# State space outputs of two channel blocks made together on the two column halves of the PE array

## The chip, the cores and the metric

The kernel runs on one core of a Trainium2 chip. The metric is the device time of one execution in microseconds (us). Times below are those of the kernel before, from three runs, and from one profiled execution with its trace.

## What is computed

The reference is one hybrid decoder block over 16 learned meta tokens and 512 tokens of width 1024: a half SwiGLU, then attention (sliding window, 16 query heads on 4 key heads, a sink per head) beside a state space layer, both gated and merged, then a second half SwiGLU and a last norm. Cut to what matters here:

```python
q, k, v, u, g_attn, g_ssm = jnp.split(hn @ w_in[i], SPLITS, axis=-1)
attn = sliding_window_attention(q, k, v, attn_sinks[i])
y = s5_ssm(u, ...)          # 32 groups of 16 channels, 64 complex states each
y = jax.nn.gelu(y)
ssm = (y @ ssm_glu_a[i]) * jax.nn.sigmoid(y @ ssm_glu_b[i])
merged = jax.nn.sigmoid(g_attn) * attn + jax.nn.sigmoid(g_ssm) * ssm
h = h + merged @ w_out[i]
```

The change touches only the end of `s5_ssm`, the GELU behind it, and the transposes that bring `y` into the layout in which the gated unit (`ssm_glu_a`, `ssm_glu_b`) reads it.

## The kernel before

All large products are made of units: 128 output columns against all tokens, as 24 steps. A weight tile is split into two parts (`whi` on ACT, line 173, `wlo` on DVE, line 174), the activations likewise (`hgh`, `hgl`), and three of the four partial products are summed in PSUM (`mm3`, line 238). A unit over all 528 columns of tokens has two matmuls of 264 columns a step; a unit over the 512 real tokens has one of 512. `step` issues a unit's matmuls, then the split of the weights for the unit two ahead (`prep_piece`), then the unit's evacuation. `mids` is a list of calls that go out between the matmuls of a unit, at evenly spaced cuts: with two of them after steps 8 and 16, with three after 6, 12 and 18. The schedule is written by hand: each engine runs its instructions in the order in which the program issues them.

The state space layer works by chunks of 8 time steps (T = 8, 64 chunks of real tokens) and by four blocks of 8 groups (128 channels, `b` from 0 to 3). For each block:

- `ssm_r(b)` brings the inputs `u` back from DRAM as `U`, with time step and channel on the partitions.
- `ssm_c(b)` makes the chunks' inputs to the states (`psS`, line 943, 8 fp32 matmuls, one for each group) and copies them to `SR` and `SI` on ACT.
- `ssm_d_(b)` runs the recurrence over the chunks on DVE and POOL; its last four instructions write the states `X` (lines 980 and 981, even groups, then odd groups).
- `ssm_e(b)` makes the outputs. For each group, two fp32 matmuls add up in `psY`: the inputs `U` against `Mt` (line 992) and the states `X` against `Qt` (line 993). The stationary operand has 64 columns, one for each chunk, so the output stands on 64 partitions. Four groups fill a PSUM bank, and ACT applies the GELU into `Y` (line 994), 64 partitions x 512.
- `ssm_f(b)` transposes `Y` back to channels on partitions, 8 transposes of 64 x 128 (`psT`, line 1002), and splits the result into `YH` (ACT, line 1004) and `YL` (DVE, line 1005), which the gated units read later.

These calls are spread as `mids` over the units `u(2)`, `u(3)`, `k(0)`, `k(1)`, `v(0)`, `v(1)`, `q0(0)`, `q0(1)` by the table `plan` (line 1041). The last `ssm_f(3)` stands behind the last unit, and the attention stage follows: there ACT and DVE split the keys (`KH`, `KL`, lines 1100 to 1104), ACT and POOL the queries (`qs`, lines 1129 and 1130), and the first scores (`ps_s`, line 1152) need all of these.

Tiles of `psS`, `psY` and `psT` come from one PSUM pool of four banks (`ax_ps`). `Y` has one buffer, `X` two, `U` four.

Of the kernel before, what the change touches and what calls it, by code (L numbers as in the profile page):

```python
# [60 lines left out]
def fr(ap):  # L61
    return ap.bitcast(F32)
# [3 lines left out]
def hybrid_block_kernel(  # L66
# [134 lines left out]
    def step2(ua, ub, mids=()):  # L201
        """Two units of which the last tile of operands comes late: it goes last in both."""
        a, b = ua[0](*take(), None), ub[0](*take(), None)
        next(a)
        for m in mids:
            m()
        prep_piece()
        next(b)
        for g in (a, b):
            for _ in g:  # L210
                pass
        ua[1]()
        prep_piece()
        ub[1]()
# [8 lines left out]
    def accumulate(seq, emit, mids):  # L223
        """One accumulation group; the callables in mids go out between its matmuls."""
# [126 lines left out]
    def ffn_units(hg, hT, n528, mm_ps, g_p, t_p, chunks, last_hook=None, first_mm=None, tail=False):  # L351
        """The units of one half-residual SwiGLU, hT += 0.5 * its output; with tail, the last chunk's
        down projection is left out and its operands are returned."""
# [118 lines left out]
    def ssm_params(ps_p):  # L472
# [114 lines left out]
        # the even groups' rows stay on the lower partitions, the odd ones' on the upper  # L587
# [145 lines left out]
    # the tensor engine's clock rises while the first loads are under way  # L733
# [27 lines left out]
    def x_in(h, d):  # L761
        """Block columns d of token half h: the transpose, then the two parts one and two blocks later."""
# [14 lines left out]
    def first_mm(p, hi, lo, mids):  # L777
        """The first two units take the first half of the tokens first, while the second is brought in."""
# [118 lines left out]
    def ev_u(b):  # L897
        """Step-major u: [channel, (step, chunk)], the two chunks of meta tokens first; by way of DRAM
        it comes back as [(7 - step, channel of the group), (group, chunk)]."""
# [84 lines left out]
    def ssm_e(b):  # L984
        u, xs = su.pop(b), sxs.pop(b)
        y = s_p.tile([64, T, GB, 16], F32, tag="Y", name="Y")
        for h in range(2):
            ps = ax_ps.tile([128, 512], F32, tag="ax", name="psY")
            for i in range(4):
                g = GB * b + 4 * h + i  # L990
                o = ps[:64, 128 * i:128 * i + 128]
                PE.matmul(out=o, lhsT=u[:, 4 * h + i, 2:NCH], rhs=Mt[:, g, :], start=True, stop=False)  # L992
                PE.matmul(out=o, lhsT=xs[:, 4 * h + i, :], rhs=Qt[:, g, 1:T + 1, :].rearrange("p t c -> p (t c)"), start=False, stop=True)  # L993
            S.activation(out=y[:, :, 4 * h:4 * h + 4, :].rearrange("k t g c -> k g t c"),
                         in_=ps[:64, :].rearrange("k (g t c) -> k g t c", g=4, t=T), func=AF.Gelu_apprx_tanh)
        sy[b] = y

    def ssm_f(b):
        y = sy.pop(b)
        ps = ax_ps.tile([128, 512], F32, tag="ax", name="psT")  # L1000
        for t in range(T):
            PE.transpose(ps[:, 64 * t:64 * t + 64], y[:, t].rearrange("k g c -> k (g c)"), ident[:64, :64])
        src = ps.rearrange("p (t k) -> p k t", t=T)
        S.activation(out=YH[:, b, :].rearrange("p (k t) -> p k t", t=T), in_=src, func=AF.Copy)
        V.tensor_tensor(out=YL[:, b, :].rearrange("p (k t) -> p k t", t=T), in0=src,
                        in1=fr(YH[:, b, :]).rearrange("p (k t) -> p k t", t=T), op=ALU.subtract)
# [27 lines left out]
    def go(f, b):  # L1034
        return lambda: f(b)
# [10 lines left out]
        (unit528(ev_v(0)), [(ssm_d_, 1), (ssm_c, 2), (ssm_e, 0)]),  # L1046
        (unit528(ev_v(1)), [(ssm_d_, 2), (ssm_c, 3), (ssm_e, 1), (ssm_f, 0)]),
        (unit512(ev_q0(0)), [(ssm_d_, 3), (ssm_e, 2), (ssm_f, 1)]),
        (unit512(ev_q0(1)), [(ssm_e, 3), (ssm_f, 2)]),
# [3 lines left out]
    ssm_f(3)  # L1053
# [31 lines left out]
    # masks, with the sign that the negated scores need  # L1085
# [6 lines left out]
    # hm[p, h]: 1 where row p of the stacked meta probabilities belongs to head h  # L1092
# [78 lines left out]
    def s2(n, c, kb):  # L1171
        """One block of keys: the probabilities' transpose."""
# [188 lines left out]
    # the last chunk's down projection by halves of the tokens, each half's norm behind the products  # L1361
# [115 lines left out]
```

## Time and profile before

| what | value |
|---|---|
| median of three runs | 1161.07 us (1159.37, 1161.07, 1162.34) |
| profiled execution, first to last instruction (span) | 1160.7 us |
| mean granted TensorE clock | 0.991 |
| DMA over the span | 108.42 MB, 93 GB/s |
| the eight GELUs (line 994) | 0.59 us each |
| the four `YH` copies, the four `YL` subtractions | 0.58 and 0.69 us each |

No other time is listed for the profiled execution than its span, which lies within the three runs' times.

In the rows of a timeline the columns are the start in us from the span's start, the duration, the engine, the line, the operation, output and inputs by the program's names, the part of the array (rows * columns), the shapes, how many were merged into the row, and in brackets how long the engine sat idle before and who ended it. PE is TensorE's matmuls, PEld its weight loads, DVE VectorE, ACT ScalarE, POOL GpSimd. One fp32 matmul of the program shows as two records with a weight load each; a transpose, and a matmul of the split (fp32r) parts, shows as one. Ends of matmuls overlap with the next one's start, so the cost of a group is read from starts, not from durations.

### The profile page before, as it was taken

The numbers are of one execution on the slowest core, as the hardware profiler recorded it, in microseconds if no ns is written. First come the engines' busy times: TensorE is split into PE (matmuls) and PEld (weight loads), VectorE is DVE, ScalarE is ACT, GpSimd is POOL, SyncE is SP. The second block draws the span as 40 slices with busy tenths as digits, with TensorE's granted clock in tenths as the row PEclk, the third lists the DMA queues.
The fourth block names the chain that finished last, engine by engine and source line by source line (L and its number), as shares of the span: only waits on it lengthen the run. The fifth ranks groups of instructions, "written<-read, shape, count | busy, mean of one in ns | idle before, by whom it ended". The sixth has DMA issues, their size and how long they took to land.

```text
span 1160.7 us, 17253 instructions
## 1 busy us (share of the span) xinstructions
PE 1141.6 (98%) x7022; PEld 1016.8 (88%) x7022; DVE 632.1 (54%) x956; ACT 410.4 (35%) x719; POOL 361.5 (31%) x488
## 2 busy tenths in 40 slices
PE   9999999999999999999999999999999999999997
PEld 7999999999999999987778778878888888888887
DVE  5446653645444363767776777564544444444454
ACT  5322232232222242446565464353322222232234
POOL 1966662543685030425454331021000000000003
PEclk7999999999999999999999999999999999999999
DMA  5533233322423246121122222432333223323221
GB/s 158 115 96 109 73 92 94 91 84 83 110 74 101 69 144 191 48 73 60 51 73 73 73 68 79 145 109 73 108 109 110 73 82 103 112 86 117 84 73 73
DMA packets 105582, 108.42 MB, mean 93 GB/s; under 512 B 7504, under 2 KB 101968, under 8 KB 105376
## 3 DMA queue, kind: packets, MB, share of 16 engines
q1 hardware_dynamic: 103104, 100.74, 27.8%
q0 software_dynamic: 2352, 6.52, 2.2%
q8 instruction: 55, 0.90, 0.3%
q14 instruction: 23, 0.19, 0.1%
q10 hardware_dynamic: 48, 0.07, 0.0%
HBM read 100.80 MB, written 5.34 MB: 91 GB/s over the span
## 4 chain that ended last, share of the span: by engine, by line
PE 88%; DVE 4%; ACT 3%; POOL 2%; issue 2%; DMA 1%; POOLq 0%; DVEq 0%; SPq 0%; ACTq 0%
PE p L238 58%; PE p L412 11%; PE p L414 8%; PE p L798 2%; PE p L1372 1%; DMA hT<-h_keep 1%; ACT E L1157 1%; POOL m L1200 1%; POOL E L1168 1%; PE psK L656 1%; PE psY L992 1%; DVE wlo L174 1%; PE ps_x L744 1%; PE psY L993 1%; PE psS L943 1%
## 5 line engine op out<-in xcount | busy, mean ns | idle before, releaser
L238 PE MATMUL p<-hgh,whi 128*128 128x264 f32 (+1 forms) x1408 | 403.4, 333 | 0.1
L238 PE MATMUL p<-hgl,whi 128*128 128x264 f32 (+1 forms) x1408 | 402.4, 332 | 0.0
L238 PE MATMUL p<-hgh,wlo 128*128 128x264 f32 (+1 forms) x1408 | 400.9, 331 | 0.5 <-DVE wlo L174 0.5
L174 DVE TENSOR_TENSOR wlo<-raw,whi 128x1024 fp32r<-128x1024 f32 (+2 forms) x192 | 254.0, 1323 | 104.5 <-ACT whi L173 102.2
L238 PEld LDWEIGHTS p<-hgh,whi 128*128 128x128 f32 x1408 | 238.5, 188 | 26.0 <-issue 1.5
L238 PEld LDWEIGHTS p<-hgh,wlo 128*128 128x128 f32 x1408 | 238.2, 188 | 24.6 <-DVE wlo L174 1.0
L238 PEld LDWEIGHTS p<-hgl,whi 128*128 128x128 f32 x1408 | 238.4, 188 | 22.4
L173 ACT ACTIVATE whi<-raw 128x1024 fp32r<-128x1024 f32 (+2 forms) x192 | 187.5, 979 | 133.1 <-PE p L414 72.2
L1388 POOL TENSOR_TENSOR acc<-acc,zq 128x256 f32<-128x256 f32 x12 | 8.9, 738 | 349.8 <-ACT zq L1381 349.7
L384 ACT ACTIVATE t<-t 128x528 f32<-128x528 f32 (+1 forms) x44 | 28.1, 639 | 164.3 <-DVE t L383 164.3
L394 ACT ACTIVATE gh<-t 128x528 fp32r<-128x528 f32 (+1 forms) x44 | 28.1, 639 | 159.2 <-DVE t L393 159.2
L432 DVE SCALAR_TENSOR_TENSOR hT<-p,hT 128x528 f32<-128x528 f32 (+1 forms) x56 | 39.1, 698 | 82.8 <-PE p L414 52.2
L412 PE MATMUL p<-gh,whi 128*128 128x264 f32 x352 | 72.8, 288 | 0.7 <-DVE hT L432 0.5
L412 PE MATMUL p<-gl,whi 128*128 128x264 f32 x352 | 71.5, 284 | 0.0
L412 PE MATMUL p<-gh,wlo 128*128 128x264 f32 x352 | 71.4, 284 | 0.0
L383 DVE TENSOR_TENSOR t<-p,r_bc 128x528 f32<-128x528 f32 (+1 forms) x44 | 30.7, 698 | 70.4 <-PE p L238 67.3
L393 DVE TENSOR_TENSOR t<-p,t 128x528 f32<-128x528 f32 (+1 forms) x44 | 30.7, 698 | 63.8 <-PE p L238 63.5
L412 PEld LDWEIGHTS p<-gh,whi 128*128 128x128 f32 x352 | 54.4, 188 | 2.3 <-issue 1.2
L414 PE MATMUL p<-gh,whi 128*128 128x512 f32 x144 | 56.0, 389 | 0.0
L414 PE MATMUL p<-gl,whi 128*128 128x512 f32 x144 | 56.0, 389 | 0.0
L414 PE MATMUL p<-gh,wlo 128*128 128x512 f32 x144 | 56.0, 389 | 0.0
L412 PEld LDWEIGHTS p<-gl,whi 128*128 128x128 f32 x352 | 54.6, 188 | 0.0
(322 smaller groups left out, 1516.1 us busy)
## 6 DMA issues: line engine op xcount, KB each, us to landing
raw<-in_ffn_w_dram SPq DMA_DIRECT2D x42, 1024.0 KB, 5.4
raw<-in_ffn_w_dram SPq DMA_DIRECT2D x24, 768.0 KB, 4.3
raw<-in_w_in_dram SPq DMA_DIRECT2D x16, 1024.0 KB, 5.5
raw<-in_ffn_w_dram SPq DMA_DIRECT2D x12, 512.0 KB, 3.5
raw<-in_w_out_dram SPq DMA_DIRECT2D x4, 1024.0 KB, 8.7
h_keep<-hT POOLq DMA_DIRECT2D x1, 2112.0 KB, 7.3
raw<-in_ssm_glu_a_dram SPq DMA_DIRECT2D x4, 512.0 KB, 3.6
raw<-in_ssm_glu_b_dram SPq DMA_DIRECT2D x4, 512.0 KB, 4.6
```

What stands on the lines that cost most here:

```text
L173: S.activation(out=hi, in_=src, func=AF.Copy)
L174: V.tensor_tensor(out=lo, in0=src, in1=fr(hi), op=ALU.subtract)
L238: PE.matmul(out=o, lhsT=w[:, k0 + k, :], rhs=sl(r, k), start=start, stop=stop)
L383: V.tensor_tensor(out=t1, in0=cell[1], in1=rb(), op=ALU.mult)
L384: S.activation(out=t1, in_=t1, func=AF.Silu)
L393: V.tensor_tensor(out=t3, in0=cell[3], in1=cell["t1"], op=ALU.mult)
L394: S.activation(out=gh, in_=t3, func=AF.Copy)
L412: PE.matmul(out=p[:, h, :HALF], lhsT=wt[:, k, :], rhs=gs[k][c][:, h, :], start=start, stop=stop)
L414: PE.matmul(out=p, lhsT=wt[:, k, :], rhs=gs[k][c].rearrange("p h c -> p (h c)"), start=start, stop=stop)
L432: V.scalar_tensor_tensor(out=hv(hT, d), in0=cell["p"], scalar=0.5, in1=hv(hT, d), op0=ALU.mult, op1=ALU.add)
L656: PE.matmul(out=ps[:16, 128 * i:128 * i + 128], lhsT=BB[:, 0, g, :], rhs=Qt[:, g, 0:T, :].rearrange("p t c -> p (t c)"), start=True, stop= ...
L798: PE.matmul(out=p[:, h, :HALF], lhsT=w[:, k, :], rhs=r[:, k, h * HALF:(h + 1) * HALF], start=(n == 0), stop=(n == 3 * ND - 1))
```

## The change

`ssm_e` now takes two neighbouring blocks, `b0` and `b0 + 1`. For each group of the pair it issues four matmuls: the `U` product of the first block, that of the second, the `X` product of the first, that of the second. The first block's output goes to PSUM partitions 0 to 63, that of the second to 64 to 127, which puts the two on the two column halves of the array (tiles of 128 rows x 64 columns, at columns 0 and 64). One GELU then covers both blocks on 128 partitions, and `Y` has 128 partitions. `ssm_f` takes a pair and one half `q` of the time steps: four transposes of 128 x 128, then for each of the two blocks one copy and one subtraction of 256 elements a partition. The calls move in `plan`: `ssm_e(0)` from `v(0)` to the first cut of `v(1)`, ahead of `ssm_d_(2)`; both halves of `ssm_f` for the first pair to `q0(0)`; `ssm_e(2)` to the middle of `q0(1)`; both halves for the second pair behind the last unit. Comments and docstrings are dropped as well, which alters nothing that runs.

```diff
-    def ssm_e(b):
-        u, xs = su.pop(b), sxs.pop(b)
-        y = s_p.tile([64, T, GB, 16], F32, tag="Y", name="Y")
+    def ssm_e(b0):
+        bs = (b0, b0 + 1)
+        us, xss = [su.pop(b) for b in bs], [sxs.pop(b) for b in bs]
+        y = s_p.tile([128, T, GB, 16], F32, tag="Y", name="Y")
         for h in range(2):
             ps = ax_ps.tile([128, 512], F32, tag="ax", name="psY")
             for i in range(4):
-                g = GB * b + 4 * h + i
-                o = ps[:64, 128 * i:128 * i + 128]
-                PE.matmul(out=o, lhsT=u[:, 4 * h + i, 2:NCH], rhs=Mt[:, g, :], start=True, stop=False)
-                PE.matmul(out=o, lhsT=xs[:, 4 * h + i, :], rhs=Qt[:, g, 1:T + 1, :].rearrange("p t c -> p (t c)"), start=False, stop=True)
+                gi = 4 * h + i
+                for first in (True, False):
+                    for e in range(2):
+                        g = GB * bs[e] + gi
+                        o = ps[64 * e:64 * e + 64, 128 * i:128 * i + 128]
+                        if first:
+                            PE.matmul(out=o, lhsT=us[e][:, gi, 2:NCH], rhs=Mt[:, g, :], start=True, stop=False, skip_group_check=True)
+                        else:
+                            PE.matmul(out=o, lhsT=xss[e][:, gi, :], rhs=Qt[:, g, 1:T + 1, :].rearrange("p t c -> p (t c)"),
+                                      start=False, stop=True, skip_group_check=True)
             S.activation(out=y[:, :, 4 * h:4 * h + 4, :].rearrange("k t g c -> k g t c"),
-                         in_=ps[:64, :].rearrange("k (g t c) -> k g t c", g=4, t=T), func=AF.Gelu_apprx_tanh)
-        sy[b] = y
+                         in_=ps.rearrange("k (g t c) -> k g t c", g=4, t=T), func=AF.Gelu_apprx_tanh)
+        sy[b0] = y
 
-    def ssm_f(b):
-        y = sy.pop(b)
+    def ssm_f(b0, q):
+        y = sy[b0]
         ps = ax_ps.tile([128, 512], F32, tag="ax", name="psT")
-        for t in range(T):
-            PE.transpose(ps[:, 64 * t:64 * t + 64], y[:, t].rearrange("k g c -> k (g c)"), ident[:64, :64])
-        src = ps.rearrange("p (t k) -> p k t", t=T)
-        S.activation(out=YH[:, b, :].rearrange("p (k t) -> p k t", t=T), in_=src, func=AF.Copy)
-        V.tensor_tensor(out=YL[:, b, :].rearrange("p (k t) -> p k t", t=T), in0=src,
-                        in1=fr(YH[:, b, :]).rearrange("p (k t) -> p k t", t=T), op=ALU.subtract)
+        for t in range(4):
+            PE.transpose(ps[:, 128 * t:128 * t + 128], y[:, 4 * q + t].rearrange("k g c -> k (g c)"), ident)
+        src = ps.rearrange("p (t e k) -> p e k t", t=4, e=2)
+        for e in range(2):
+            oh = YH[:, b0 + e, :].rearrange("p (k t) -> p k t", t=T)[:, :, 4 * q:4 * q + 4]
+            ol = YL[:, b0 + e, :].rearrange("p (k t) -> p k t", t=T)[:, :, 4 * q:4 * q + 4]
+            S.activation(out=oh, in_=src[:, e], func=AF.Copy)
+            V.tensor_tensor(out=ol, in0=src[:, e], in1=fr(oh), op=ALU.subtract)
...
-        (unit528(ev_v(0)), [(ssm_d_, 1), (ssm_c, 2), (ssm_e, 0)]),
-        (unit528(ev_v(1)), [(ssm_d_, 2), (ssm_c, 3), (ssm_e, 1), (ssm_f, 0)]),
-        (unit512(ev_q0(0)), [(ssm_d_, 3), (ssm_e, 2), (ssm_f, 1)]),
-        (unit512(ev_q0(1)), [(ssm_e, 3), (ssm_f, 2)]),
+        (unit528(ev_v(0)), [(ssm_d_, 1), (ssm_c, 2)]),
+        (unit528(ev_v(1)), [(ssm_e, 0), (ssm_d_, 2), (ssm_c, 3)]),
+        (unit512(ev_q0(0)), [(ssm_d_, 3), (ssm_f, 0, 0), (ssm_f, 0, 1)]),
+        (unit512(ev_q0(1)), [(ssm_e, 2)]),
     ]
...
-    ssm_f(3)
+    ssm_f(2, 0)
+    ssm_f(2, 1)
```

Three places show what moves. The first is PE's queue where the first output block begins (in `v(0)` before); these are rows of the kernel before.

```order
L238 MATMUL p<-hgl,whi 128x264 x2
L238 MATMUL p<-hgh,wlo 128x264 x2
L992 MATMUL psY<-Mt,U 64x128
L993 MATMUL psY<-Qt,X 64x128
L992 MATMUL psY<-Mt,U 64x128
```

And these are rows of PE's queue at the first output block of the changed kernel (in `v(1)`, after six steps), with the semaphores that an instruction waits for.

```order
L238 MATMUL p<-hgl,whi 128x264 x2
L238 MATMUL p<-hgh,wlo 128x264 x2
L999 MATMUL psY<-Mt,U 64x128 [waits DMASW4_49,DMASW5_49,DMASW3_49,DMASW6_49,DMASW2_49,DMASW7_49,DMASW1_49,DMASW0_49] x2
L1001 MATMUL psY<-Qt,X 64x128
L1001 MATMUL psY<-Qt,X 64x128 [waits DVE_49]
L999 MATMUL psY<-Mt,U 64x128 x2
L1001 MATMUL psY<-Qt,X 64x128
```

Instructions of the two blocks now alternate, and the first two that read the second block's states (`X`, even groups, then odd groups) wait for DVE; the waits for DMA are for `Mt`, built long before.

The second place is ACT's queue at the end of the stage, from the last GELUs to the first key splits. Before:

```order
L994 ACTIVATE Y<-psY 64x4x8x16 x2
L1004 ACTIVATE YH<-psT 128x512
L173 ACTIVATE whi<-raw 128x1024
L1004 ACTIVATE YH<-psT 128x512
L1100 ACTIVATE KH<-kT 64x544
```

The same place of ACT's queue in the changed kernel, from the weight split ahead of the last GELUs on:

```order
L173 ACTIVATE whi<-raw 128x1024
L1003 ACTIVATE Y<-psY 128x4x8x16 x2
L173 ACTIVATE whi<-raw 128x1024
L1017 ACTIVATE YH<-psT 128x64x4 x4
L1113 ACTIVATE KH<-kT 64x544
```

Between the last transposes and the first key split stand four copies of 256 elements a partition in place of one of 512.

The third place is DVE's queue between the states of block 2 and those of block 3. Before:

```order
L981 TENSOR_TENSOR X<-a_5386,a_5387 64x4x64
L1005 TENSOR_TENSOR YL<-psT,YH 128x512
L174 TENSOR_TENSOR wlo<-raw,whi 128x1024
L930 TENSOR_TENSOR vT<-p,r_bc 128x528
L961 TENSOR_TENSOR a_5515<-SR,pr 128x264
```

In the changed kernel, from the end of block 3's states on:

```order
L980 TENSOR_TENSOR X<-a_5499,a_5500 64x4x64
L981 TENSOR_TENSOR X<-a_5501,a_5502 64x4x64
L1018 TENSOR_TENSOR YL<-psT,YH 128x64x4 x4
L174 TENSOR_TENSOR wlo<-raw,whi 128x1024
L1042 SCALAR_TENSOR_TENSOR tq_5563<-p,r_bc 128x512
```

The split of the first outputs stood ahead of the recurrence of block 3 (lines 961 to 981) and now stands behind it.

More of the change, by code (lines that the diff above doesn't have):

```diff
@@ L1032, in ev_q0, with go @@
         return f
-    def go(f, b):
-        return lambda: f(b)
+    def go(f, *a):
+        return lambda: f(*a)
     step(*unit528(ev_u(0)), hold=True)
```

## The prediction

> **What bounds the kernel now.** I read the page first: which engine is busy, and what the chain that ended last is made of.
>
> ```profile
> PE 1141.6 (98%) x7022; PEld 1016.8 (88%) x7022; DVE 632.1 (54%) x956; ACT 410.4 (35%) x719; POOL 361.5 (31%) x488
> ...
> PE 88%; DVE 4%; ACT 3%; POOL 2%; issue 2%; DMA 1%; POOLq 0%; DVEq 0%; SPq 0%; ACTq 0%
> ```
>
> TensorE is busy for 98% of the span and makes 88% of the chain. A busy PE is not a PE at its peak, so I then took the table by stage, for the stretch that the change rewrites (from the unit `v(0)` to the last transposes), and the rows of its two tiles.
>
> ```profile
> 469.37:514.33 44.96, 44.96 (x339) 40.08 (x337) 28.17 (x53) 16.50 (x34) 15.74 (x25) 1.00 0.16 48
> ...
> L992 PEld LDWEIGHTS psY<-Mt,U x64: 133/137/137, 475.6 to 508.4; 128*64 128x64 f32 x64
> L992 PE MATMUL psY<-Mt,U x64: 272/273/323, 475.6 to 508.5; 128*64 128x128 f32 x64
> L993 PE MATMUL psY<-Qt,X x64: 272/272/273, 475.9 to 508.7; 128*64 128x128 f32 x64
> L1002 PE MATMUL psT<-ident,Y x32: 221/223/273, 491.2 to 514.2; 64*128 64x64 f32 x32
> ```
>
> In this stretch (columns: length, busy time of PE, PEld, DVE, ACT and POOL, granted clock, DMA share, GB/s) PE never waits and has its full clock, DVE is busy for 28.2 of 45.0 us, ACT for 16.5. So time is won here only by giving PE less to do, and what PE saves reaches the end unless a wait takes its place. `psY` is 128 records on half of the columns (64 fp32 matmuls, two records each); `psT` is 32 records on half of the rows. Next, what one block of each costs inside the stream of ordinary 512-column matmuls:
>
> ```profile
> 495.44 0.40 PE L238 MATMUL p<-hgl,whi 128*128 128x512 f32 x1
> 495.68 0.40 PE L238 MATMUL p<-hgh,wlo 128*128 128x512 f32 x1
> 496.00 0.43 PE L992 MATMUL psY<-Mt,U 128*64 128x128 f32 x2
> 496.27 0.38 PE L993 MATMUL psY<-Qt,X 128*64 128x128 f32 x2
> ...
> 499.33 0.38 PE L993 MATMUL psY<-Qt,X 128*64 128x128 f32 x2
> 499.64 0.50 PE L238 MATMUL p<-hgh,whi 128*128 128x512 f32 x1
> 499.98 0.39 PE L238 MATMUL p<-hgl,whi 128*128 128x512 f32 x1
> ...
> 500.91 0.39 PE L238 MATMUL p<-hgh,wlo 128*128 128x512 f32 x1
> 501.23 0.71 PE L1002 MATMUL psT<-ident,Y 64*128 64x64 f32 x8
> 501.86 0.50 PE L238 MATMUL p<-hgh,whi 128*128 128x512 f32 x1
> 502.20 0.39 PE L238 MATMUL p<-hgl,whi 128*128 128x512 f32 x1
> ```
>
> Ordinary matmuls start 0.23 us apart. From 495.68 to 499.98 lie two such steps (0.46) and one `psY` block: 4.30 - 0.46 = **3.84 us**, four times 15.4. Inside it 28 records start between 496.27 and 499.33: 0.109 each, so 32 take 3.50 and 0.34 goes to entering and leaving. From 500.91 to 502.20: 1.29 - 0.46 = **0.83 us** for a `psT` block, four times 3.3.
>
> **The change part by part.** *Output matmuls.* There are as many as before, 64 instructions or 128 records, now in two blocks of 64 whose instructions alternate between the halves. If the halves run side by side, the time of two records is that of one. It can't be less: the two records of one instruction use the same half and keep their 0.109. A block is then 32 x 0.109 + 0.34 = 3.84, two are 7.7, and 15.4 - 7.7 = **7.7 us** are saved. If nothing overlaps, a block is 64 x 0.109 + 0.34 = 7.34, two are 14.7, and 0.7 is saved (two entries). No row of before shows a second half, so its pitch lies between these ends, or above the upper one if changing halves costs something. One thing that could bind is loading weights:
>
> ```profile
> 496.00 0.19 PEld L992 LDWEIGHTS psY<-Mt,U 128*64 128x64 f32 x2 [0.37 <-issue]
> ...
> 472.29 1.90 PE L943 MATMUL psS<-U,Wt 128*128 128x66 f32 x16
> ```
>
> The first two loads of a block last 0.19 together and one lasts 0.137, so the second began 0.053 after the first; `psS`, with twice the columns to load and short streams, runs at (1.90 - 0.27)/15 = 0.109 a record, again 0.055 for 64 columns. Side by side, two loads fall on every 0.109: just enough. I take the full overlap, since every load in these rows already runs under a matmul of the same rows of the array.
>
> The Trainium skill, "TensorEngine Tiling (Array Packing)", section "Key Properties", says that changing the tiling mode drains the engine, while different tiles run weight loads and matmuls in parallel. For the first this trace has 0.34 us a block; no run here shows the second. Its "TensorE: Matmul & The Clock Gate", "Measured speedup vs the span model", has 2.38 for three column tiles; scaled to two that is 1.59, and my estimate by it is two blocks of 4.74, 5.9 saved in place of 7.7.
>
> *Transposes.* 32 of 64 rows become 16 of 128 x 128. Four such stand elsewhere in the trace:
>
> ```profile
> 154.43 0.41 PE L238 MATMUL p<-hgh,wlo 128*128 128x264 f32 x2
> 154.67 0.60 PE L671 MATMUL psW<-ident,Pb 128*128 128x128 f32 x4
> 155.02 0.49 PE L238 MATMUL p<-hgh,whi 128*128 128x264 f32 x2
> 155.35 0.28 PE L238 MATMUL p<-hgl,whi 128*128 128x264 f32 x1
> ```
>
> From 154.43 to 155.35 lie four ordinary steps of 0.122 (0.49) and the four transposes: 0.43, with no gap at either end. Four groups make 1.7 for 3.3: **1.6 us** saved.
>
> *GELU and the split.* ACT has four GELUs for eight, and eight copies of 256 elements for four of 512; DVE likewise eight short subtractions. Both engines idle beside PE here, so I count nothing, but for the last group (below). The DMA queues and POOL keep their order.
>
> *The new wait.* `ssm_e(0)` now also needs block 1's states, one cut into `v(1)`.
>
> ```profile
> 479.33 0.42 DVE L981 TENSOR_TENSOR X<-a,a 64x256 f32<-64x256 f32 x1
> ```
>
> DVE's order up to there is unchanged, so the last write of block 1's states still ends at 479.75. Before, `psS` of block 2 (472.29) stands 12 steps into `v(0)`, a step being two matmuls of 0.122, 0.243 in all, so `v(0)` starts at 469.37. Without `psY` in it, `v(0)` lasts 24 steps (5.84) and 16 records of `psS` (1.75): to 476.96. Six steps (1.46) and the entry (0.1) lead to 478.5; the first matmul on odd-group states of block 1 comes 0.8 later when overlapped, at 479.3. It waits some **0.5 us**, `psY` and all of `v(1)` behind it. If nothing overlaps, it comes at 480.1 and waits for nothing. The second pair:
>
> ```profile
> 493.55 0.69 DVE L1005 TENSOR_TENSOR YL<-psT,YH 128x512 fp32r<-128x512 f32 x1 [4.46 <-ACT YH L1004]
> 494.50 1.23 DVE L174 TENSOR_TENSOR wlo<-raw,whi 128x1024 fp32r<-128x1024 f32 x1 [0.26 <-ACT whi L173]
> ...
> 502.14 0.42 DVE L981 TENSOR_TENSOR X<-a,a 64x256 f32<-64x256 f32 x1
> 505.31 0.43 PE L992 MATMUL psY<-Mt,U 128*64 128x128 f32 x2
> ```
>
> Before, the states were done at 502.56, 2.75 ahead of PE. PE now comes 7.1 earlier: three blocks (11.5) and two `psT` (1.7) less, one block with its wait (4.3) and two transpose groups (0.9) more, and four steps (0.9) later in its unit. It needs odd states at 505.3 - 7.1 + 0.8 = 499.0. DVE's 4.46 us of waiting for `YH` go, since that split moves behind these states. From the weight split to the last state DVE needs 8.06 (494.50 to 502.56), and by my count it starts that at 490.4, when ACT has finished `psS` of block 3 and the weights: 498.5. I count nothing; 0.5 of margin is thin.
>
> *The end of the stage.* The last transposes now make four short copies on ACT, ahead of attention's key and query splits.
>
> ```profile
> 513.69 0.71 PE L1002 MATMUL psT<-ident,Y 64*128 64x64 f32 x8
> 514.44 0.60 ACT L1004 ACTIVATE YH<-psT 128x512 fp32r<-128x512 f32 x1
> 514.93 0.65 ACT L1100 ACTIVATE KH<-kT 64x544 fp32r<-64x544 f32 x1
> 518.42 9.84 POOL L1130 TENSOR_TENSOR qs<-tq,qs 64x512 fp32r<-64x512 f32 x6 [14.81 <-ACT qs L1129]
> 525.58 0.33 PE L1152 MATMUL ps_s<-KH,qs 128*128 128x144 f32 x1 [0.84 <-POOL qs L1130]
> ```
>
> Before, `KH` starts 1.24 after the first transpose, POOL follows ACT, and PE waits 0.84 for POOL at 525.58. Now the first group is done 0.6 after its start (the 0.60 of `psW` above), and four copies at half of the 0.49 between `YH` and `KH` follow: `KH` at about 1.65, some **0.45 us** later with the gaps between copies, which PE pays there in full. If POOL catches up, it costs nothing.
>
> *Sum*: 7.7 + 1.6 - 0.5 - 0.45 = 8.3 us (7.7 + 1.6 = 9.3 without the two waits). The profiled span is 1160.7 and runs go down to 1159.4, so nothing to speak of lies around it; the median is 0.3 above it. 1161.1 - 8.3 = **1152.8 us**.
>
> **The rivals.** *Half an overlap.* In all rows the next load starts as the matmul before it starts. If the other half's load keeps this rule, a matmul of the other half begins 0.055 late and the next of its own 0.109 after it: four records take 0.33 in place of 0.44. A block is 16 x 0.33 + 0.34 = 5.6, two 11.2: 4.2 saved; with 1.6, a wait of 0.2 and the 0.45, 5.2 in all: 1155.9. For it: no row shows a load more than one matmul ahead. Against: all these rows are loads into the columns that the running matmul uses, and the other half's columns are free.
>
> *The halves take turns.* The change doesn't do what it says: 0.7 + 1.6 - 0.45 = 1.8 saved, 1159.3. For it: nothing in the trace ever ran two matmuls at once.
>
> *Loads wait for the other half.* If a load for one half waits until the other half's matmul has ended, each change of half costs 0.055. There are 31 a block, 62 in all: 3.4 us, 1.6 more than the 1.8: 1162.7. Against: loads here run under matmuls. The Trainium skill, "TensorE: Matmul & The Clock Gate", "The mechanism", has such a rule (a load overlaps a matmul in flight only when the row group differs), and both halves share all rows; for loads of the same tile the trace disagrees (496.00 to 499.33: 0.109 a record, not 0.109 + 0.055).
>
> *Slower: each change of half drains PE* as a change of tile shape does. Entering and leaving cost 0.34, so one change 0.17; 62 cost 10.5 against 1.8: 8.7 slower, **1169.8**. It decides from 0.03 us a change on, where 62 eat the 1.8. For it: every change of shape in these rows has its gap. Against: the shape, 128 x 64, stays the same inside a block.
>
> **How the numbers follow.** Full overlap 0.46, half 0.20, taking turns 0.19, waiting loads 0.06, draining 0.09. About 0.3% (3.5 us) is what a measurement of this kernel can tell from no change: below 1157.6 are the first two, 0.66; within are the next two, 0.25; above is the drain, 0.09. The likeliest gives the time. The range starts from it without the two waits (1151.8) less 0.8 for the spread of runs, 1151.0, and goes up over half an overlap to taking turns (1159.3) with the spread of 1.2: 1160.5. Outside are the last two cases, 0.15.
>
> **What would show it.** Right: `psY` records starting in pairs, a block of about 3.8 us (4.3 with the wait) for twice the work; `psT` groups of 0.43 without gaps; a wait of about 0.5 on DVE's `X` in the first block and none in the second; the wait on POOL's `qs` up from 0.84 to 1.3. Half an overlap: blocks of 5.6. Taking turns: blocks of 7.3, 0.109 a record. Draining: gaps at each change, blocks above 12. The forecast is wrong if the blocks exceed 5, or if they shrink and a wait for `X`, `qs` or weights grows by as much.

## The result, and the profile after

The changed kernel takes 1152.74 us (median of six runs, 1151.1 to 1156.33) where the kernel before, run beside it, takes 1162.02 (1159.37 to 1162.34): a ratio of 0.9926, 95% interval 0.9912 to 0.9941. The two medians differ by 9.3 us; the ratio gives 8.6, and its interval 6.9 to 10.2. One execution of the repeated changed kernel further down ran its matmuls at less than half their pace throughout (2571 us); it was the profiled one, and no number is taken from its profile.

From the page of the changed kernel, the busy times and the chain that ended last:

```profile
PE 1130.5 (98%) x7006; PEld 1006.9 (88%) x7006; DVE 632.7 (55%) x960; ACT 408.8 (36%) x719; POOL 360.5 (31%) x488
...
PE 86%; DVE 5%; ACT 4%; issue 2%; POOL 2%; DMA 0%; POOLq 0%; DVEq 0%; SPq 0%; ACTq 0%
```

PE is busy for 11.1 us less and still bounds the kernel, though 2% of the chain has gone from it to DVE and ACT. The spans of the two profiles (1160.7 and 1150.2) differ by 10.5 us, and not all of that is the change: in the first 20 us both kernels run the same instructions, and the table by windows has another clock for them (before, then after; the granted clock is the third number from the right).

```profile
0.00:20.00 20.00, 17.66 (x71) 13.22 (x72) 9.67 (x21) 11.70 (x24) 3.24 (x14) 0.68 0.71 214
```

```profile
0.00:20.00 20.00, 18.02 (x81) 13.40 (x81) 10.38 (x23) 11.50 (x24) 3.22 (x14) 1.00 0.71 215
```

PE is 3.1 us ahead by 60 us and still 3.2 at 460 us, where the change begins. The clock column points at the reason, but its 1.00 after is too high: there, too, the matmuls begin at a slow pace. A pair of transposes of one kind (`ps_x`) takes 0.63 us while the pace is slow and 0.38 afterwards; in the changed kernel the pace rises at about 16 us, in the kernel before it is still slow at 23.67 (changed kernel, then before).

```profile
15.16 0.63 PE L744 MATMUL ps_x<-ident,xb 128*128 128x128 f32 x2
...
16.48 0.38 PE L744 MATMUL ps_x<-ident,xb 128*128 128x128 f32 x2
```

```profile
23.67 0.63 PE L744 MATMUL ps_x<-ident,xb 128*128 128x128 f32 x2
```

When the pace rises differs from one execution to the next and not with the change: at 460 us the profiles of the experiments stand between 0.8 us ahead of this one and 3.4 behind it, and the kernel before with its keys on POOL (below) is only 0.4 behind. From here on I count in one way: number PE's matmuls from the end of the program, subtract the start times of the same matmul in two traces, and take off what that difference was at 460 us. By this count the changed kernel is **8.6 us** ahead after the rewritten stage, 6.3 after the first 20 us of attention, and 7.3 at the end. The stage itself, from the same first instruction to the same last one as in the window shown of before (44.96):

```profile
466.26:502.66 36.40, 36.16 (x322) 32.81 (x320) 30.27 (x56) 14.58 (x31) 16.56 (x25) 1.00 0.19 59
```

The second output block, in the timeline of the changed kernel (start, duration, engine, line, operation, array tile, shapes, records merged):

```profile
495.00 0.40 PE L238 MATMUL p<-hgh,wlo 128*128 128x512 f32 x1
495.32 0.44 PE L999 MATMUL psY<-Mt,U 128*64 128x128 f32 x4
495.59 0.39 PE L1001 MATMUL psY<-Qt,X 128*64 128x128 f32 x4
495.81 0.39 PE L999 MATMUL psY<-Mt,U 128*64 128x128 f32 x4
...
498.97 0.50 PE L238 MATMUL p<-hgh,whi 128*128 128x512 f32 x1
499.30 0.40 PE L238 MATMUL p<-hgl,whi 128*128 128x512 f32 x1
```

Each row now merges four records (two instructions, one for each half) where it merged two, and the rows still start 0.22 apart: two records in the time of one. The block costs 499.30 - 495.00 - 0.46 = **3.84 us** for twice the work. The first block costs 4.53, since it waits. The wait in the view of the tile `psY`, and the last write of the second pair's states in the timeline:

```profile
  DVE X L981: 0.7, 2
```

```profile
495.21 0.42 DVE L981 TENSOR_TENSOR X<-a,a 64x256 f32<-64x256 f32 x1
```

In the changed kernel, idle time ahead of `psY` that ended with DVE's `X` is 0.7 us in two waits, all in the first block; the second pair's states are done at 495.63, 0.3 after its block began with products that don't need them. The four groups of transposes cost 0.43, 0.45 and, for the last two together, 0.88 (502.97 - 501.63 - 0.46 below): 1.76 for 3.33. Then the end of the stage, from the last ordinary matmul ahead of the last transposes on:

```profile
501.63 0.40 PE L238 MATMUL p<-hgh,wlo 128*128 128x512 f32 x1
501.87 1.04 PE L1012 MATMUL psT<-ident,Y 128*128 128x128 f32 x8
502.50 0.39 ACT L1017 ACTIVATE YH<-psT 128x256 fp32r<-128x256 f32 x1 [1.87 <-PE psT L1012]
502.92 0.42 DVE L1018 TENSOR_TENSOR YL<-psT,YH 128x256 fp32r<-128x256 f32 x1 [0.16 <-ACT YH L1017]
502.97 0.39 PE L238 MATMUL p<-hgl,whi 128*128 128x512 f32 x1
503.38 0.66 ACT L1017 ACTIVATE YH<-psT 128x256 fp32r<-128x256 f32 x2 [0.49 <-DVE YL L1018]
...
504.59 0.39 ACT L1017 ACTIVATE YH<-psT 128x256 fp32r<-128x256 f32 x1 [0.55 <-DVE YL L1018]
504.87 0.65 ACT L1113 ACTIVATE KH<-kT 64x544 fp32r<-64x544 f32 x1
...
511.68 1.95 DVE L174 TENSOR_TENSOR wlo<-raw,whi 128x1024 fp32r<-128x1024 f32 x1 [0.66 <-ACT whi L173]
...
514.66 0.30 PE L1165 MATMUL ps_s<-KH,qs 128*128 128x144 f32 x1 [1.54 <-DVE mn L1168]
```

ACT and DVE take turns on the same `psT` tile: the copy for the second block waits for DVE's subtraction of the first (0.49, 0.55). `KH` starts 3.00 us after the first of the last transposes, where it was 1.24. PE pays first at its third score (`ps_s`, the product with `KH`), 12.79 after those transposes; before it was 10.71 (524.40 - 513.69). At the fourth score about 1.0 of that comes back, because the kernel before waits there 0.84 for `qs` and the changed one no longer does. But DVE and ACT stay behind, and at the third score of the next group PE waits again, where the kernel before doesn't:

```profile
522.43 0.39 PE L1165 MATMUL ps_s<-KH,qs 128*128 128x272 f32 x1 [0.76 <-DVE mn L1168]
```

By the count above PE loses 0.3 at the first two scores and 1.8 at the third, regains 1.0 at the fourth, and loses 1.2 around this wait: 2.3 in all.

### The profile page after: what moved, and what is told of

Its sections match the earlier page's. It is cut to its first block, busy times and chain, and to the rows that moved or that the text cites. A ratio compares the mean times of both kernels' runs of the same rounds, so it can differ in the third digit from the quotient of the medians.

```text
span 1150.2 us, 17220 instructions
## 1 busy us (share of the span) xinstructions
PE 1130.5 (98%) x7006; PEld 1006.9 (88%) x7006; DVE 632.7 (55%) x960; ACT 408.8 (36%) x719; POOL 360.5 (31%) x488
## 4 chain that ended last, share of the span: by engine, by line
PE 86%; DVE 5%; ACT 4%; issue 2%; POOL 2%; DMA 0%; POOLq 0%; DVEq 0%; SPq 0%; ACTq 0%
PE p L238 58%; PE p L412 11%; PE p L414 9%; PE p L798 1%; ACT E L1170 1%; PE p L1385 1%; POOL m L1213 1%; POOL E L1181 1%; DVE wlo L174 1%; PE psK L656 1%; ACT whi L173 1%; PE ps_x L744 1%; PE ps_t L1189 1%; ACT qs L1142 0%; PE pv L1224 0%
## 5 line engine op out<-in xcount | busy, mean ns | idle before, releaser
L1181 POOL TENSOR_TENSOR E<-E,den 128x512 f32<-128x512 f32 (+1 forms) x20 | 28.5, 1431 | 84.9 <-DVE den L1176 57.4
```

The source lines that it names most:

```text
L1181: G.tensor_tensor(out=E[:, :, c:c + w], in0=E[:, :, c:c + w], in1=den.unsqueeze(2).to_broadcast([128, 4, w]), op=ALU.mult)
```

## The experiments

All are edits of the changed kernel unless said. "By trace" is the count described above, against the first profile of the changed kernel, at the end of the program, positive where the experiment is ahead.

| kernel | first, second output block (us) | by trace | median (us) | ratio to before, 95% |
|---|---|---|---|---|
| changed, first time | 4.53, 3.84 | 0 | 1152.74 | 0.9912 to 0.9941 |
| changed, again | no profile used | | 1153.59 | 0.9907 to 0.9946 |
| changed, a third time | 4.47, 3.85 | -1.6 (see the end) | 1154.49 | 0.9908 to 0.9946 |
| block order | 6.19, 6.19 | -4.2 | 1158.06 | 0.9952 to 0.9981 |
| pair order | 4.47, 3.89 | -0.3 | 1154.77 | 0.9917 to 0.9950 |
| runs of four | 4.98, 4.67 | -1.3 | 1155.76 | 0.9925 to 0.9965 |
| one copy | 4.34, 3.84 | +1.4 | 1151.78 | 0.9896 to 0.9930 |
| copies first | 4.40, 3.84 | +1.1 | 1152.56 | 0.9905 to 0.9935 |
| old transposes | 4.34, 3.84 | -0.4 | 1155.80 | 0.9916 to 0.9958 |
| one copy, later pair | 3.84, 3.84 | +1.9 | 1150.06 | 0.9887 to 0.9924 |
| the same, again | 3.84, 3.84 | +1.9 | 1150.39 | 0.9886 to 0.9922 |
| that, keys on POOL | 3.84, 3.84 | -0.3 | 1152.31 | 0.9904 to 0.9928 |
| before, keys on POOL | four of 3.83 | -8.4 (before: -7.3) | 1162.08 | 0.9995 to 1.0014 |

**The base again.** No edit. Its use is the spread: three medians of this one kernel lie between 1152.7 and 1154.5, so differences under 2 us are read from the traces.

> The changed kernel unaltered, as the base of the next ones. Output blocks of 4.5 (0.7 of it a wait for X) and 3.85 us, as in its first profile. If the 3.1 us by which the first 25 us differed between the two profiles was the clock at the start of one execution and not the change, the spread of the spans here covers it, and the part of the time that the change explains is 7 us: 8.5 won in the stage, 2.2 given back at attention's start, 0.85 regained later.

**What makes the halves run side by side.** Three orders of the same matmuls on the same tiles. Block order (the two products of a group stand behind these loops, `U` first):

```diff
-            for i in range(4):
-                gi = 4 * h + i
-                for first in (True, False):
-                    for e in range(2):
-                        g = GB * bs[e] + gi
+            for e in range(2):
+                for i in range(4):
+                    gi = 4 * h + i
+                    g = GB * bs[e] + gi
...
```

> Same tiles and halves, but in each bank all eight matmuls of the first block come before all eight of the second. Theory A (the halves run side by side only where neighbours in PE's queue are on different halves, so the alternation is what wins): only three changes of half a block can overlap, a block is 64 x 0.109 + 0.34 less at most 3 x 0.11 = 7.0 to 7.3 us; two are 14.0 to 14.6 against 8.4, less no wait for X: about 5.8 us slower than the changed kernel, 1158.5. Theory B (each half works through a long queue of its own): blocks of 3.85 as before, same time within 0.5. Theory C (the gain is from merging, not from overlap): cannot be, if A or B holds; it would give the changed kernel's time too, with 0.055 a record.

Pair order:

```diff
-                for first in (True, False):
-                    for e in range(2):
+                for e in range(2):
+                    for first in (True, False):
```

> For each group both matmuls of the first block, then both of the second: the halves change every two instructions and not at each. Theory A in its strict form (the records of all halves start in one order, each after the one before it): U0 at 0 and 0.109, X0 at 0.218 and 0.327, U1 at 0.327 and 0.436, X1 at 0.545 and 0.654, so a period of 0.654 for 8 records, a block of 8 x 0.654 + 0.34 = 5.6 us, two 11.2 against 8.4: about 3 us slower, 1155.7. Theory A in a loose form (one instruction may pass ahead of the next, or a few are looked at): period 0.436, blocks of 3.85, same time within 0.5. Theory B: the same 3.85.

The block order gave blocks of 6.19: neither theory. Its timeline at the change from the first half to the second, inside one bank:

```profile
476.00 0.38 PE L998 MATMUL psY<-Qt,X 128*64 128x128 f32 x2
476.22 0.44 PE L997 MATMUL psY<-Mt,U 128*64 128x128 f32 x4
476.44 0.44 PE L998 MATMUL psY<-Qt,X 128*64 128x128 f32 x4
476.71 0.38 PE L997 MATMUL psY<-Mt,U 128*64 128x128 f32 x2
```

Rows of two records are one half alone; the two rows of four are both together. In the single records the second half starts at 476.224, 6 ns behind the 13th of the first half's 16 (476.218), and so ahead of three records that come before it in the program:

```
first half (its last four):  476.218  476.327  476.436  476.545
second half (its first):     476.224  476.384  476.493  476.602  476.711
```

Three such changes win (7.34 - 6.19)/3 = 0.384 each, 3.5 records. The pair order, with four records on a half, loses nothing but 0.05, which refutes a strict order of all starts (5.6). Together they suggest a new theory, D: PE starts a matmul on a free half if it is among about the next four records, even past others that wait for the other half. It was put to the test by runs of eight records:

```diff
-            for i in range(4):
+            for i2 in range(2):
+                for e in range(2):
+                    for i in (2 * i2, 2 * i2 + 1):
...
```

> Runs of four instructions (eight records) on one half, then four on the other, so 7 changes of half a block. The block order gave 6.19 a block where none of both theories put it: 7.34 less three changes of 0.384 each, 3.5 records, and the trace has the second half's first matmul start together with the 13th of the first half's 16 records. New theory D: PE looks some four records ahead of the one that runs; a half whose next records lie within that starts, and a half that has none among them stands idle. Then each change wins 0.384: 7.34 - 7 x 0.384 = 4.65 us a block; two 9.3, less the wait for X: about 0.9 slower than the changed kernel. If the look-ahead were counted in instructions or groups and not in records, or the alternation at bank borders alone mattered: 6.19, or 3.85.

The second block, which waits for nothing:

```profile
498.80 0.40 PE L238 MATMUL p<-hgh,wlo 128*128 128x512 f32 x1
...
503.93 0.39 PE L238 MATMUL p<-hgl,whi 128*128 128x512 f32 x1
```

503.93 - 498.80 - 0.46 = 4.67, where D said 4.65. So the alternation is needed, but only to within about four records.

**Where the gain went at attention's start.** One copy and one subtraction a group instead of two each:

```diff
-        for e in range(2):
...
-            S.activation(out=oh, in_=src[:, e], func=AF.Copy)
-            V.tensor_tensor(out=ol, in0=src[:, e], in1=fr(oh), op=ALU.subtract)
+        oh = YH[:, b0:b0 + 2, :].rearrange("p e (k t) -> p e k t", t=T)[:, :, :, 4 * q:4 * q + 4]
+        ol = YL[:, b0:b0 + 2, :].rearrange("p e (k t) -> p e k t", t=T)[:, :, :, 4 * q:4 * q + 4]
+        S.activation(out=oh, in_=src, func=AF.Copy)
+        V.tensor_tensor(out=ol, in0=src, in1=fr(oh), op=ALU.subtract)
```

> ssm_f takes one copy and one subtraction of 512 elements for both blocks of a group in place of two each of 256, which takes away ACT's two waits for DVE in each pair. Theory: these waits (0.49 and 0.55) and the doubled number of copies are why KH started 3.0 us after the first of the last transposes in place of 1.24; with one copy a group it starts at 0.63 + 2 x 0.6 = 1.85 after, 1.1 to 1.2 us earlier, and most of that comes back at PE's waits for mn and qs: 1151.5 to 1151.9 where the changed kernel has 1152.7. Rival: the loss at attention's start is DVE's and POOL's own work there (wlo of 1.95 us, qs on POOL), which KH's start does not govern: KH earlier, no time back, same within 0.3.

And as many copies as in the changed kernel, but both ahead of both subtractions:

```diff
         for e in range(2):
-            S.activation(out=oh, in_=src[:, e], func=AF.Copy)
-            V.tensor_tensor(out=ol, in0=src[:, e], in1=fr(oh), op=ALU.subtract)
+            S.activation(out=oh[e], in_=src[:, e], func=AF.Copy)
+        for e in range(2):
+            V.tensor_tensor(out=ol[e], in0=src[:, e], in1=fr(oh[e]), op=ALU.subtract)
```

> As many copies and subtractions as in the changed kernel (two each a group, of 256 elements), but both copies go out before both subtractions, so that ACT has no wait for DVE between them. Tells the wait from the number of copies. Theory: the waits are the larger part: the first group is done 0.63 after the first of the last transposes, its two copies take 0.7 to 0.8, the second group's the same, KH starts at 2.1 in place of 3.0 (one copy a group: 1.61), and of the 1.4 us that KH's start won with one copy, and the 1.2 that came back, about two thirds appear here: 0.8 us faster than the changed kernel. Rival: the number of copies is what costs; KH within 0.2 of 3.0.

The end of the stage with one copy, then with the copies first:

```profile
503.63 1.04 PE L1012 MATMUL psT<-ident,Y 128*128 128x128 f32 x8
...
504.26 1.08 ACT L1016 ACTIVATE YH<-psT 128x512 fp32r<-128x512 f32 x2 [1.86 <-PE psT L1012]
...
505.24 0.64 ACT L1113 ACTIVATE KH<-kT 64x544 fp32r<-64x544 f32 x1
...
512.06 2.13 DVE L174 TENSOR_TENSOR wlo<-raw,whi 128x1024 fp32r<-128x1024 f32 x1 [0.66 <-ACT whi L173]
...
515.22 0.30 PE L1165 MATMUL ps_s<-KH,qs 128*128 128x144 f32 x1 [0.57 <-DVE mn L1168]
```

```profile
504.21 1.04 PE L1012 MATMUL psT<-ident,Y 128*128 128x128 f32 x8
504.84 1.21 ACT L1016 ACTIVATE YH<-psT 128x256 fp32r<-128x256 f32 x4 [1.87 <-PE psT L1012]
...
505.92 0.66 ACT L1113 ACTIVATE KH<-kT 64x544 fp32r<-64x544 f32 x1
...
515.98 0.30 PE L1165 MATMUL ps_s<-KH,qs 128*128 128x144 f32 x1 [0.79 <-DVE mn L1168]
```

`KH` starts 1.61 and 1.71 after the first transpose (3.00), and the third score 11.59 and 11.77 after it (12.79). With the waits gone and the count of copies the same, 1.0 of the 1.2 us comes back: it was the turn-taking on one PSUM tile, not the number of instructions. I had put two thirds on it; it is five sixths.

**The wait for `X`.** One copy, and the first pair six steps later, behind `ssm_d_(2)` in `plan`:

```diff
-        (unit528(ev_v(1)), [(ssm_e, 0), (ssm_d_, 2), (ssm_c, 3)]),
+        (unit528(ev_v(1)), [(ssm_d_, 2), (ssm_e, 0), (ssm_c, 3)]),
```

> One copy a group, and ssm_e(0) at the second cut of v(1), after six more steps (1.46 us), in place of the first. The first output block's wait for X (0.5 to 0.7) goes: block 3.85 in place of 4.3 to 4.5; nothing else moves but ssm_d_(2) on POOL and DVE, which is issued ahead of it. 0.5 faster than one copy alone: 1151.3, and its profile 0.5 ahead of that one after the stage. Against: psS of block 3 (third cut) and the states that hang on it come no later, so the second block should stay at 3.85; if it waits for X(3), the gain is given back there.

The first block falls to 3.84, the second stays there, and the kernel is 0.5 ahead of one copy alone by trace, as expected. This is the best version: run again beside the unaltered changed kernel, on one chip, the two medians are 1150.39 and 1154.49.

> The changed kernel unaltered, on the same chip and beside the next one, to compare the two without a chip between them: 1152.7, as at first.

> One copy a group and the later first pair, beside the unaltered changed kernel. From the traces it should be 1.9 faster (1.2 at attention's start, 0.7 at the wait for X): 1150.8. If the 2.7 by which its first median lay lower was luck of the chip or of the starts, the two come out within 0.5.

By trace it is 1.9 ahead both times; the 4.1 between the last two medians holds more than that, and the section on the hardware shows a part of it.

**The transposes.** `ssm_f` as before the change, 8 transposes of 64 rows for one block, now from the lower or upper partitions of `Y`:

```diff
-        for t in range(4):
-            PE.transpose(ps[:, 128 * t:128 * t + 128], y[:, 4 * q + t].rearrange("k g c -> k (g c)"), ident)
+        r = slice(64 * e, 64 * e + 64)
+        for t in range(T):
+            PE.transpose(ps[:, 64 * t:64 * t + 64], y[r, t].rearrange("k g c -> k (g c)"), ident[r, r])
...
```

> The new output blocks, but transposes and split as in the kernel before: per block 8 transposes of 64 rows (now from partitions 0 to 63 or 64 to 127 of the merged Y), one copy and one subtraction of 512. Prices the new transposes: 4 x 0.83 in place of 1.76, so 1.55 us more of PE; ACT's ping-pong with DVE is gone as in the one-copy kernel, which gives about 1.2 back at attention's start: the changed kernel's time within 0.6, and 1.5 slower than the one-copy kernel. If the two last blocks, which lie on different row halves and follow each other in PE's queue, overlap as the column halves do over about four records, their 1.66 becomes 1.4.

The first two groups cost 0.84 each, as in the kernel before. The last two follow each other in PE's queue on different row halves:

```profile
505.69 0.39 PE L238 MATMUL p<-hgh,wlo 128*128 128x512 f32 x1
506.01 1.02 PE L1013 MATMUL psT<-ident,Y 64*128 64x64 f32 x16
...
507.30 0.39 PE L238 MATMUL p<-hgl,whi 128*128 128x512 f32 x1
```

Together 1.15 by these rows, not 1.69: one entry and exit less (0.34) and an overlap of 0.2, some three records of 0.062, as between column halves. A transpose is one record and an fp32 matmul two, so about the same number of records in both cases speaks for a reach that is counted in records and not in instructions. So the new transposes win 1.57 over the kernel before, but only 1.07 over old ones side by side. Against one copy alone this kernel is 1.7 behind at the end, 1.05 of it by the end of attention's start and 0.5 from a wait at 751 us, of which more below.

**What is left at attention's start.** Even with one copy, 0.9 to 1.0 us is lost there against the kernel before. In that version ACT works without a gap from the copies to `whi`, so its four `KH` copies were moved to POOL, which idles; and the same move was made in the kernel before.

```diff
-            S.activation(out=KH[r, 2 * m + e, :], in_=t[r], func=AF.Copy)
-            S.activation(out=KH[o, 2 * m + e, :], in_=t[r], func=AF.Copy)
+            [S.activation(out=KH[x, 2 * m + e, :], in_=t[r], func=AF.Copy) for x in (r, o)] if m else \
+                [G.tensor_copy(KH[x, 2 * m + e, :], t[r]) for x in (r, o)]
```

> The version with one copy and the later pair, and with the four KH copies of the first two key heads on POOL in place of ACT. Tests where the rest of the loss at attention's start sits: after one copy a group about 1.0 of the 2.2 us is left. Theory: ACT's chain there (two YH, four KH, four qs, VB, whi, 7.8 us without a gap) is what DVE's first E and so PE's ps_s wait for; POOL is idle for 10.2 us ahead of its qs. With KH on POOL from about 498, at some 1.25 us a copy by its own rows (COPY 128x264 0.61), qs, VB and whi come 2 to 2.6 earlier on ACT, and the wait of ps_s for mn in this place (0.57) and the gaps around it go: 1.0 to 1.3 faster than that version, 1149. Rival: POOL's copies are slower than that or slow DVE beside them (wlo took 2.13 beside POOL's qs and 1.22 without), POOL's own qs come later, and the time is the same or worse by up to 1.

> The kernel before with the same move of KH to POOL and nothing else: how much of that move has to do with this change. Before, PE lost 0.84 for POOL's qs and up to 1.7 for mn at the same place. If ACT's chain was late there too, 0.5 to 1 is won here as well, 1161.3; if only the change made ACT late, the same time within 0.3.

The rival held. POOL made the keys early, and its `qs` began 2.3 us after the first of the last transposes (500.82) in place of 5.1. The rows of POOL and DVE, and PE's third score, in the first of these kernels:

```profile
495.63 3.59 POOL L1114 CAST KH<-kT 64x544 fp32r<-64x544 f32 x4
...
503.14 6.48 POOL L1143 TENSOR_TENSOR qs<-tq,qs 64x512 fp32r<-64x512 f32 x4 [3.92 <-ACT qs L1142]
503.49 1.51 DVE L1116 TENSOR_TENSOR KL<-kT,KH 64x544 fp32r<-64x544 f32 x1
505.01 1.72 DVE L1117 TENSOR_TENSOR KL<-kT,KH 64x544 fp32r<-64x544 f32 x1
...
512.82 0.30 PE L1165 MATMUL ps_s<-KH,qs 128*128 128x144 f32 x1 [0.98 <-DVE mn L1168]
```

All four `KL` now run beside POOL's `qs` and take 1.5 to 1.7 us each; in the changed kernel they took 0.72 and were all but done when `qs` began. The third score comes 12.00 after the first transpose in place of 11.59. In the kernel before the move changes nothing in the median, and by trace it too is later by about 1.3 there. So ACT's lateness is not what is left to win in this way: what ACT gives up, DVE loses beside POOL.

What the remaining 0.9 to 1.0 is made of can be read from rows but was not tried apart. The same place of the kernel before, and then the one `qs` of POOL during which `wlo` begins with one copy (512.06 above):

```profile
520.28 1.67 POOL L1130 TENSOR_TENSOR qs<-tq,qs 64x512 fp32r<-64x512 f32 x1
...
521.76 1.27 DVE L174 TENSOR_TENSOR wlo<-raw,whi 128x1024 fp32r<-128x1024 f32 x1 [0.52 <-ACT whi L173]
...
524.40 0.23 PE L1152 MATMUL ps_s<-KH,qs 128*128 128x144 f32 x1
```

```profile
511.83 1.29 POOL L1143 TENSOR_TENSOR qs<-tq,qs 64x512 fp32r<-64x512 f32 x1
```

Counted from the first of the last transposes, `wlo` starts at 8.43 with one copy and at 8.07 before: 0.36, about what `KH` is late. And it takes 2.13 where it took 1.27: 0.86. In both kernels `wlo` begins while a `qs` runs on POOL, and in both it ends about 1.08 us after that `qs` has ended (521.95 to 523.03, and 513.12 to 514.19); in the changed kernel it is 1.09. So its length goes by how much of that `qs` is left when it begins: 0.19 us before, 1.06 with one copy. That makes the 0.86 a matter of where the two engines stand to each other and not of more work; no run here moves that alone.

## Why the prediction was right

The number was 1152.8 and the median 1152.74, and the direction, the range and the likeliest case held. The closeness is better than the terms deserve. Point by point:

- **Output matmuls, 7.7.** The two blocks without waits would be 7.69 for 15.36: full overlap to within 0.02. The price per record (0.109) and the 0.34 for entering and leaving held. The loads were no limit, but not for the reason worked out: those of the two halves start together and not 0.055 apart. Half an overlap, turns, waiting loads and drains are refuted by the blocks. The scaled estimate from the Trainium skill's "TensorE: Matmul & The Clock Gate", "Measured speedup vs the span model" (5.9 saved) was too low: two column halves gave 2.0. The rule of its "The mechanism", that a load overlaps a matmul in flight only when the row groups differ (just ahead of it the section also allows a load into a background weight buffer), does not hold as it stands for these column halves, which share all rows: in the records of the block shown, loads and matmuls of the two halves start within 8 ns of each other.
- **The rivals' common picture** was an order in which records start one after the other over both halves. That was wrong in kind: block order and runs of four show some four records of look-ahead, out of program order. The alternation written in the change is finer than needed (pair order loses 0.05 a block).
- **Transposes, 1.6.** Measured 1.57, groups of 0.44 without gaps.
- **The new wait, 0.5.** It came where it was put and cost 0.69, 0.63 and less (0.5) in three profiles; the later first pair removes it.
- **The second pair's margin, 0 counted.** Held: no wait, 3.84. The last write of `X` ended at 495.63, 0.4 ahead of the first product that needs it (496.03).
- **The end of the stage, 0.45: the failing step.** It cost 2.3 (8.6 to 6.3). "Four copies at half of the 0.49" took each copy by its own length and overlooked that copy and subtraction of one `psT` tile wait for each other, 1.0 to 1.2 of it. Most of the rest, by the rows, it had at nothing: `wlo` on DVE met a `qs` of POOL that had longer to run. The prediction also took PE's wait for `qs` to grow; instead that wait fell away, and DVE's `mn`, which stands behind `wlo`, became the one that PE waits for. The place was right, the releaser and the size were not.

By trace the sum is 8.6 - 2.3 = 6.3 in this place, and 7.3 at the end: in the kernel before, PE loses another 0.8 in the output projection to a weight split that comes late, a wait that the changed kernel's profile doesn't have. In the kernel before:

```profile
758.00 0.50 PE L238 MATMUL p<-hgh,wlo 128*128 128x512 f32 x1 [0.52 <-DVE wlo L174]
```

ACT splits these weights behind `hgh`, which needs DVE's `hT`, and that waits for `h_keep`, the hidden state read back from DRAM (before, then after):

```profile
753.72 0.69 DVE L1334 SCALAR_TENSOR_TENSOR hT<-p,hT 128x512 f32<-128x512 f32 x1 [7.23 <-DMA hT<-h_keep]
```

```profile
742.44 0.69 DVE L1347 SCALAR_TENSOR_TENSOR hT<-p,hT 128x512 f32<-128x512 f32 x1 [5.57 <-DMA hT<-h_keep]
```

This wait is 6.9 to 7.2 us in the three profiles that lose here (0.8 in the kernel before, 0.6 in that kernel with keys on POOL, 0.5 with the old transposes) and 5.6 to 6.1 in ten others, which lose nothing. All three have the old transposes, so no run tells whether the read comes late by chance or because of them.

Against 8.3 forecast, the trace thus gives 6.3 to 7.3 to the change, around the lower end of the interval's 6.9 to 10.2. The ratios of the three measurements of the changed kernel give 8.6, 8.5 and 8.5 us. Why they give more than the trace is not settled; the first 25 us alone put single profiled executions up to 4.2 apart. So that 1152.74 came out at 1152.8 is partly luck: the end of the stage cost 1.85 more than forecast, and the medians show a gain that the traces don't.

## What to carry to other kernels

Two products that each use half of the array's columns cost the time of one here if they are issued within about four matmul records of each other; in a coarser order only about 3.5 records overlap at each change of half. When a PSUM tile is read by two engines, issue all reads of the one before those of the other, or one instruction each: alternating reads in the program become waits in both queues. And work moved off a late engine wins nothing if another engine then runs slower beside it: look at the durations there, and at what runs beside them, not only at the gaps.

## What the runs showed of the hardware

The start of the second half ahead of three earlier matmuls of the first (block order, above) had not been expected. The Trainium skill, "TensorE: Matmul & The Clock Gate", "The mechanism", has matmuls start strictly in program order and loads pulled ahead over 64 instructions; here matmuls on another column half, and on another row half in the old transposes, passed earlier ones, and over only three or four records.

Turns between ACT and DVE on one tile: the waits are written into the program's semaphores, so no run here shows the two reading one bank at once. The Trainium skill, "PSUM — Partial Sum Buffer", "PSUM bank collisions raise a hardware error", says that engines may not access the same bank of a partition in the same cycle, which would be a reason for them.

Behind a wait the clock can drop. In the third run of the changed kernel PE waits 1.74 us for `mn` near 589 us, as the first did (1.71) without harm; this time the wait, and the windows of the wait and behind it, read:

```profile
589.38 0.39 PE L1165 MATMUL ps_s<-KH,qs 128*128 128x272 f32 x1 [1.74 <-DVE mn L1168]
```

```profile
588.00:590.30 2.30, 0.93 (x7) 0.80 (x7) 2.08 (x7) 0.95 (x4) 0.00 (x0) 1.00 1.02 330
590.30:593.76 3.46, 3.46 (x12) 2.70 (x9) 2.32 (x10) 2.71 (x9) 1.50 (x2) 0.51 0.15 50
```

For 3.46 us the granted clock is 0.51, and 1.6 us are lost, the whole of that run's -1.6 in the table. The version with keys on POOL shows the same dip at the same wait, which makes 1.5 of its 2.2 behind the version that it was made from. Eleven other profiles have this wait as well, 1.71 to 1.76 us, without the dip; that the wait brings it on is likely but not shown. The Trainium skill, "TensorE: Matmul & The Clock Gate", "What's actually happening", has a gate that halves the clock by windows of about 3.4 us after an idle one; the length and the half agree, but here the gap was 1.74 us with PE busy for 0.93 of the 2.30 around it. So a wait of that size is followed by nothing in one execution and by a loss of 1.6 us in another, which may be a part of the spread of 1150.5 to 1156.8 among the changed kernel's runs.
